# Two attention stacks: even and odd heads' scores in turn, transposed attention outputs from values held on column halves

## The chip, the cores and the metric

The kernel runs on one core of a Trainium2 chip. The metric is the device time of one execution in microseconds, as the median of several; one execution was also taken with the profiler, and its trace is what is read below.

## The reference

Two blocks follow each other on one sequence of 256 tokens and 1024 channels, each with two layers. A layer of the first block is a feed-forward network, a mixer and a second feed-forward network; a layer of the second block is a mixer of four branches and a feed-forward network. Cut to the attention, which is all that the change touches:

```python
# first block, mixer: 12 heads in 3 groups of dilated causal windows, 4 stick-breaking heads; head size 64
p = jnp.exp(s - m)                                  # s = q.k / 8, masked by window and dilation
o = einsum(p, v) / denom                            # per group; lse = m + log(denom)
w_grp = softmax(stack(lses)); o_dil = sum(w_grp * outs)
w = where(past, exp(log_beta + after), 0); o_sb = einsum(w, v)
y = gate_dil * (o_dil @ w_proj_dil) + gate_sb * (o_sb @ w_proj_sb)

# second block, mixer: 8 query heads on 2 key/value heads in branches a and d
k_cmp, v_cmp = gelu(blocks @ w1) @ w2               # 15 compressed keys and values
o_a = ga0 * attend(compressed) + ga1 * attend(selected) + ga2 * attend(window)
o_b, o_c = conformer_conv(b_in), pool_mixer(c_in)
o_d = sliding window attention with one sink logit per head in the denominator
mix = sum_n sigmoid(h @ w_gate)_n * (o_n @ w_branch[n]); x = x + norm(mix @ w_o)
```

With 256 tokens the selected branch sees every causal key, so it needs no selection.

## The kernel before

Everything is held on chip but the weights, which stream from memory once. Tokens are handled as two tiles of 128 (`t` is 0 or 1). Each product with a weight matrix runs in three TensorE passes over a high and a low part of both operands (lines 184 to 186, and 204 to 219 for the feed-forward layers of the first block). `chunk` loads a piece of a weight matrix (DMA, line 107), ScalarE makes its high part `wh` (110) and VectorE its low part `wl` (111). There are six buffers for such pieces, so loads and halving run ahead of TensorE by at most six pieces.

Attention runs in plain float32. A float32 matmul is two records in the trace, a transpose, a bfloat16 matmul or a weight pass is one. Per token tile and head the steps are: a mask is added into a PSUM bank by a bfloat16 matmul with the identity (434, 538 to 542), the scores follow into the same bank (440, 483, 546, 829), VectorE takes the row maximum (442, 549), ScalarE makes the exponentials `e` with their sums (558), TensorE transposes them (155), VectorE or ScalarE copies the result to `pt`, and `pt` is the stationary operand of the product with the values (468, 500, 572), which move with 64 columns. The output lies tokens by channels, and is then scaled by the reciprocal of the sums (469, 812, 848, 856 and 857). `split_T` transposes it (155) and splits it into high and low parts for the next weight product.

Queries and keys lie with channels on partitions, two heads to a tile: an even head on the lower 64 rows of the array, an odd head on the upper 64 rows. In `attn`, called six times a layer (once for each tile in the sliding window branch `oD`, twice for each in `oA`), all even heads are served first, then all odd ones, in banks of four heads at `t` = 0 and of two at `t` = 1. In `attend1` one head of each group is served at a time.

The compressed keys come from `compress`: 16 steps of three passes (723 to 725) with 32 stationary columns; then a gelu, small transposes, a product (757), eight copies by GpSimd that lay out `hv` (764) and a product with `hv` stationary (768).

A scheduler builds the order of each engine's instructions from the code, with priorities and an estimate of durations of its own. Each engine then runs its list in order. Weight products stand between the attention steps in TensorE's list and cover the time in which VectorE and ScalarE work on a bank. PSUM has four banks for weight products (`lin`) and four for everything else (`aux`). The convolution of branch b is 240 multiply-adds on VectorE (866), and they share the stretch of the second mixer with the softmax steps and with the halving of weights.

Of the kernel before, what the change touches and what calls it, by code (L numbers as in the profile page):

```python
# [9 lines left out]
F32R = mybir.dt.float32r  # L10
# [15 lines left out]
def body(tc, ctx, I, C, out, upto=99):  # L26
# [371 lines left out]
    def attend1(qkn, vs):  # L398
        QT = [None, None]
        oTs = []  # L400
        for t in range(2):
# [25 lines left out]
            oc = unit("oc")  # L427
            for j in range(4):
                groups = [[0, 1, 2]] if t == 0 else [[0, 1], [2]]
                ps_l, mx, sm = [], stat(4), stat(4)  # L430
                for gi, gs in enumerate(groups):
                    n = len(gs) * nk * P
                    ps = aux_ps()[:, :n]
                    nc.tensor.matmul(ps, identb, dilm[t][:, gs[0]:gs[-1] + 1, :].rearrange("p g k -> p (g k)"),
                                     start=True, stop=False)
# [10 lines left out]
                V.tensor_scalar(mx[:, 2:3], mx[:, 0:1], -0.125, None, op0=OP.mult)  # L446
                pts = []
                for gi, gs in enumerate(groups):
                    n = len(gs) * nk * P
                    e = unit("e")[:, :n]  # L450
                    S.activation(e, ps_l[gi], AF.Exp, bias=mx[:, 2:3], scale=0.125, accum_out=sm[:, gi:gi + 1])
# [11 lines left out]
                if len(groups) == 2:  # L463
                    V.tensor_add(sm[:, 0:1], sm[:, 0:1], sm[:, 1:2])
                V.reciprocal(sm[:, 2:3], sm[:, 0:1])
# [8 lines left out]
            for par in range(2):  # L474
                o = par * 64
                z = aux_ps()[:, :n]
                nc.tensor.matmul(z[:, n - 256:], identb, sbm[:, None, :].to_broadcast([P, 2, P]), start=True, stop=False)
                for kt in range(nk):
                    for jj in range(2):
# [3 lines left out]
                        nc.tensor.matmul(z[:, c0:c0 + P], k_, q_, start=False, stop=(kt == nk - 1 and jj == 1))  # L483
                S.activation(es[par], z, AF.Abs)
                zs.append(z)
# [11 lines left out]
            for j in range(4):  # L497
                for kt in range(nk):
                    c0 = kt * 256 + (j // 2) * P
                    nc.tensor.matmul(po[:, j * 64:(j + 1) * 64], ws[j % 2][:, c0:c0 + P],  # L500
                                     vs[kt][:, 768 + j * 64:768 + (j + 1) * 64], start=kt == 0, stop=kt == nk - 1)
            V.tensor_copy(oc[:, 256:512], po)
            o = split_T("c", [oc])
            o1, o2 = XT(), XT()
            o1.h, o1.l, o2.h, o2.l = o.h[:2], o.l[:2], o.h[2:], o.l[2:]
# [19 lines left out]
    def attn(t, qT, kTf, vf, window, sink=None):  # L525
# [3 lines left out]
        mx, ng, dn = stat(8), stat(8), stat(8)  # L529

        def scores(h0):
            par = h0 % 2
            hs = list(range(h0, h0 + 2 * per, 2))
            n = per * nk * P
            ps = aux_ps()[:, :n]
# [619 lines left out]
```

## Time and profile before

| | us |
|---|---|
| three executions | 2177.4, 2174.1, 2173.64 |
| median | 2174.1 |
| the profiled execution's own time | 2173.62 |
| its span in the trace | 2171.8 |
| TensorE busy in the span | 2142.1 (99%) |
| VectorE busy | 1567.7 (72%) |
| ScalarE busy | 1159.0 (53%) |
| GpSimd busy | 38.7 (2%) |

Mean granted TensorE clock of the span: 0.998 of full speed. A row of the timeline gives start, duration, engine, line, operation, output and inputs, the shape and the count of records run together, and in brackets the idle time before them and what ended it. The durations of matmuls overlap, so what one costs is the distance from its start to the next start on TensorE.

### The profile page before, as it was taken

The numbers are of one execution on the slowest core, as the hardware profiler recorded it, in microseconds if no ns is written. First come the engines' busy times: TensorE is split into PE (matmuls) and PEld (weight loads), VectorE is DVE, ScalarE is ACT, GpSimd is POOL, SyncE is SP. The second block draws the span as 40 slices with busy tenths as digits, with TensorE's granted clock in tenths as the row PEclk, the third lists the DMA queues.
The fourth block names the chain that finished last, engine by engine and source line by source line (L and its number), as shares of the span: only waits on it lengthen the run. The fifth ranks groups of instructions, "written<-read, shape, count | busy, mean of one in ns | idle before, by whom it ended". The sixth has DMA issues, their size and how long they took to land.

```text
span 2171.8 us, 30964 instructions
## 1 busy us (share of the span) xinstructions
PE 2142.1 (99%) x11824; PEld 1824.8 (84%) x11824; DVE 1567.7 (72%) x2395; ACT 1159.0 (53%) x1766; POOL 38.7 (2%) x55
## 2 busy tenths in 40 slices
PE   7999999999999999999999999999999999999998
PEld 6888888888888888888887888889987888888997
DVE  6875556786677555577757997678976898577983
ACT  5654545554555455555545554456655554446652
POOL 0000000000000000000000000000000000000000
PEclk9999999999999999999999999999999999999999
DMA  8666534666666654366666632456656643355653
GB/s 252 202 193 186 193 97 139 192 192 190 192 188 187 188 191 127 118 183 185 190 188 198 200 117 78 155 172 200 192 188 191 216 140 113 107 184 175 186 179 121
DMA packets 250821, 373.86 MB, mean 172 GB/s; under 512 B 14768, under 2 KB 123696, under 8 KB 250672
## 3 DMA queue, kind: packets, MB, share of 16 engines
q1 hardware_dynamic: 250096, 371.48, 55.8%
q8 instruction: 93, 1.52, 0.3%
q0 software_dynamic: 576, 0.39, 0.1%
q14 instruction: 56, 0.46, 0.1%
HBM read 371.17 MB, written 1.05 MB: 171 GB/s over the span
## 4 chain that ended last, share of the span: by engine, by line
PE 93%; DVE 3%; issue 1%; DMA 1%; ACT 1%; POOL 1%; SPq 0%; POOLq 0%; DVEq 0%; ACTq 0%
PE lin L186 17%; PE lin L184 17%; PE lin L185 16%; PE lin L218 15%; PE lin L219 8%; PE aux L155 4%; PE lin L206 3%; PE lin L205 3%; PE lin L204 3%; PE aux L546 2%; PE aux L572 1%; DVE wl L111 1%; PE aux L440 1%; PE aux L468 1%; ACT wh L110 0%
## 5 line engine op out<-in xcount | busy, mean ns | idle before, releaser
L111 DVE TENSOR_TENSOR wl<-raw,wh 128x1024 fp32r<-128x1024 f32 (+1 forms) x688 | 835.1, 1217 | 407.5 <-ACT wh L110 399.8
L110 ACT ACTIVATE wh<-raw 128x1024 fp32r<-128x1024 f32 (+1 forms) x688 | 723.2, 1055 | 557.0 <-PE lin L186 314.1
L218 PE MATMUL lin<-x,wh 128*128 128x512 f32 x1408 | 494.9, 396 | 0.0
L219 PE MATMUL lin<-x,wl 128*128 128x256 f32 x1408 | 395.3, 281 | 0.0
L184 PE MATMUL lin<-wh,x 128*128 128x512 f32 (+2 forms) x896 | 350.0, 391 | 0.0
L185 PE MATMUL lin<-wl,x 128*128 128x512 f32 (+2 forms) x896 | 348.2, 389 | 1.5 <-DVE wl L111 1.5
L186 PE MATMUL lin<-wh,x 128*128 128x512 f32 (+2 forms) x896 | 348.2, 389 | 1.0 <-DVE rs L1057 0.8
L218 PEld LDWEIGHTS lin<-x,wh 128*128 128x128 f32 x1408 | 264.5, 188 | 61.6
L219 PEld LDWEIGHTS lin<-x,wl 128*128 128x128 f32 x1408 | 266.4, 189 | 0.5 <-DVE wl L111 0.4
L186 PEld LDWEIGHTS lin<-wh,x 128*128 128x128 f32 x896 | 168.9, 189 | 34.5 <-DVE rs L1057 1.6
L185 PEld LDWEIGHTS lin<-wl,x 128*128 128x128 f32 x896 | 168.9, 189 | 33.0 <-DVE wl L111 1.9
L184 PEld LDWEIGHTS lin<-wh,x 128*128 128x128 f32 x896 | 168.8, 189 | 32.6 <-ACT wh L110 0.4
L186 PE MATMUL lin<-wh,lo 128*128 128x512 f32 x480 | 188.6, 393 | 0.4 <-DVE lo L147 0.4
L184 PE MATMUL lin<-wh,hi 128*128 128x512 f32 x480 | 187.2, 390 | 0.0
L185 PE MATMUL lin<-wl,hi 128*128 128x512 f32 x480 | 187.0, 390 | 0.0
L205 PE MATMUL lin<-x,wh 128*128 128x256 f32 x576 | 163.2, 283 | 0.0
L206 PE MATMUL lin<-x,wl 128*128 128x256 f32 x576 | 163.0, 283 | 0.0
L204 PE MATMUL lin<-x,wh 128*128 128x256 f32 x576 | 163.0, 283 | 0.0
L205 PEld LDWEIGHTS lin<-x,wh 128*128 128x128 f32 x576 | 110.6, 192 | 0.1
L204 PEld LDWEIGHTS lin<-x,wh 128*128 128x128 f32 x576 | 110.6, 192 | 0.1
L206 PEld LDWEIGHTS lin<-x,wl 128*128 128x128 f32 x576 | 110.6, 192 | 0.0
L186 PEld LDWEIGHTS lin<-wh,lo 128*128 128x128 f32 x480 | 90.1, 188 | 19.5 <-DVE lo L147 1.3
(317 smaller groups left out, 2774.0 us busy)
## 6 DMA issues: line engine op xcount, KB each, us to landing
raw<-in_ffn_w_up_dram SPq DMA_DIRECT2D x168, 512.0 KB, 4.3
raw<-in_ffn_w_down_dram SPq DMA_DIRECT2D x132, 512.0 KB, 4.2
raw<-in_w_in_dram SPq DMA_DIRECT2D x132, 512.0 KB, 4.1
raw<-in_ffn_w_gate_dram SPq DMA_DIRECT2D x88, 512.0 KB, 4.4
raw<-in_w_gate_dram SPq DMA_DIRECT2D x64, 512.0 KB, 3.8
raw<-in_w_branch_dram SPq DMA_DIRECT2D x32, 512.0 KB, 4.4
raw<-in_w_out_dram SPq DMA_DIRECT2D x16, 512.0 KB, 4.4
raw<-in_nsa_cmp_w_dram SPq DMA_DIRECT2D x16, 512.0 KB, 4.3
```

Of the source, the lines that this page charges most:

```text
L110: S.activation(wh, raw, AF.Copy)
L111: V.tensor_sub(wl, raw, wh.bitcast(F32))
L155: nc.tensor.transpose(p[:, i * P:(i + 1) * P], s, ident)
L184: nc.tensor.matmul(ps, xt.h[k], w[0], start=start, stop=False)
L185: nc.tensor.matmul(ps, xt.h[k], w[1], start=False, stop=False)
L186: nc.tensor.matmul(ps, xt.l[k], w[0], start=False, stop=stop)
L204: nc.tensor.matmul(o, wh, xh, start=k == 0 and i % 2 == 0, stop=False)
L205: nc.tensor.matmul(o, wh, xl, start=False, stop=False)
L206: nc.tensor.matmul(o, wl, xh, start=False, stop=k == 7 and i % 2 == 1)
L218: nc.tensor.matmul(o, wh, x, start=k == 0, stop=False)
L219: nc.tensor.matmul(o[:, :T], wl, x[:, :T], start=False, stop=k == 7)
L546: nc.tensor.matmul(pv[:, i, kt * P:(kt + 1) * P], q_, kTf(kt, h), start=False, stop=(i == per - 1 and kt == nk - 1))
```

## The change

Scores: even and odd heads get a bank each at the same time, and their matmuls are issued in turn (attention of both blocks and the compressed scores). A bank holds the same heads as before.

Values: the product is turned round. A head's or key head's 64 value columns are stationary, on the lower or the upper 64 columns of the array, and the transposed probabilities move. In `attn` one such matmul serves the four query heads of a key head with 512 moving columns; in `attend1` one serves one head, with 128. The output lies channels by tokens, and `split` alone makes the operand of the next weight product; the transposes of `oc`, `od` and `oa` go. The three parts of branch a add up in one PSUM bank, as the value product of the compressed part becomes four of 128 columns.

Scaling: the probabilities are multiplied by gate and reciprocal of the sum on VectorE after the exponential and before the transposes; the scaling of the outputs goes.

Compressed keys: high and low parts of the inputs stand side by side as 64 stationary columns, so two passes do for three; their sum is taken after the transposes by VectorE, the gelu is done by ScalarE when it writes `hv`, so GpSimd's copies go; the block moves behind the keys' transposes of tile 0. The rows of `w_branch_2` for branches a and d are put in the new order on the host, before the launch.

```diff
-            oc = unit("oc")
-            for j in range(4):
-                groups = [[0, 1, 2]] if t == 0 else [[0, 1], [2]]
-                ps_l, mx, sm = [], stat(4), stat(4)
...
+                    pss = [aux_ps()[:, :n] for _ in js]
...
-                        h = gg * 4 + j
...
-                            nc.tensor.matmul(ps[:, c0:c0 + P], qk(h, False, t), qk(h, True, kt), start=False,
-                                             stop=(gg == gs[-1] and kt == nk - 1))
-                    V.tensor_reduce(mx[:, gi:gi + 1], ps, op=OP.max, axis=AX.X)
-                    ps_l.append(ps)
+                            for ps, j in zip(pss, js):
+                                h = gg * 4 + j
+                                nc.tensor.matmul(ps[:, c0:c0 + P], qk(h, False, t), qk(h, True, kt), start=False,
+                                                 stop=(gg == gs[-1] and kt == nk - 1))
...
+                    V.tensor_scalar(e, e, sm[:, 2:3], None, op0=OP.mult)
...
-                            pts.append((u[:, c0:c0 + P], vs[kt][:, h * 64:h * 64 + 64]))
...
-                po = aux_ps()[:, :64]
-                for i, (a, b) in enumerate(pts):
-                    nc.tensor.matmul(po, a, b, start=i == 0, stop=i == len(pts) - 1)
-                V.tensor_scalar(oc[:, j * 64:(j + 1) * 64], po, sm[:, 2:3], None, op0=OP.mult)
+                            pts.append((vs[kt][:, h * 64:h * 64 + 64], u[:, c0:c0 + P]))
...
+                js = (2 * jp, 2 * jp + 1)
+                pts = [probs(j, *r) for j, r in zip(js, scores(js))]
+                if po is None:
+                    po = aux_ps()[:, :256]
+                for i in range(len(pts[0])):
+                    for par in range(2):
+                        nc.tensor.matmul(po[par * 64:par * 64 + 64, jp * P:(jp + 1) * P], *pts[par][i],
+                                         start=i == 0, stop=i == len(pts[0]) - 1)
+            ob = big("c", "hl", F32R)
+            hi, lo = ob[:, 0:512], ob[:, 512:1024]
+            split(po, hi[:, 0:256], lo[:, 0:256])
...
-            V.tensor_copy(oc[:, 256:512], po)
-            o = split_T("c", [oc])
...
+                        nc.tensor.matmul(po[par * 64:par * 64 + 64, jj * P:(jj + 1) * P], vs[kt][:, v0:v0 + 64],
+                                         ws[par][:, c0:c0 + P], start=kt == 0, stop=kt == nk - 1)
+            split(po, hi[:, 256:512], lo[:, 256:512])
...
+            for i in range(per):
                 for kt in range(nk):
-                    nc.tensor.matmul(pv[:, i, kt * P:(kt + 1) * P], q_, kTf(kt, h), start=False,
-                                     stop=(i == per - 1 and kt == nk - 1))
+                    for par, pv in enumerate(pvs):
+                        h = h0 + 2 * i + par
+                        q_ = qT[par * 64:par * 64 + 64, (h // 2) * P:(h // 2 + 1) * P]
+                        nc.tensor.matmul(pv[:, i, kt * P:(kt + 1) * P], q_, kTf(kt, h), start=False,
+                                         stop=(i == per - 1 and kt == nk - 1))
...
+            V.reciprocal(f[:, hh], dn[:, hh])
+            if gate is not None:
+                V.tensor_tensor(f[:, hh], f[:, hh], gate[:, hh], op=OP.mult)
+            for sl, ev in r:
+                V.tensor_tensor(ev, ev, f[:, sl][:, :, None].to_broadcast([P, per, nk * P]), op=OP.mult)
+
+        def turned(g, kt):
+            u = unit("pt")
+            pt = transposed([es[4 * g + r][:, kt * P:(kt + 1) * P] for r in range(4)])
...
-                    nc.tensor.matmul(po[:, h * 64:h * 64 + 64], u[:, c0:c0 + P], vf(kt, h), start=kt == 0, stop=kt == nk - 1)
...
+        us = {}
+        for h0 in range(0, 8, 2 * per):
+            scores(h0)
+        for kt in range(nk):
+            for g in range(2):
+                us[g, kt] = turned(g, kt)
+        for kt in range(nk):
+            for g in range(2):
+                nc.tensor.matmul(po[g * 64:(g + 1) * 64], vf(kt, g), us[g, kt], start=first and kt == 0,
+                                 stop=last and kt == nk - 1)
...
-            split(A, ah, al)
...
+                split(A[:, q * 256:(q + 1) * 256].rearrange("p (s n) -> p s n", s=8), v[:, :, 0], v[:, :, 1])
+                ahl += [x[:, i * 64:(i + 1) * 64] for i in range(8)]
...
-                    a = slice(s * 32, (s + 1) * 32)
-                    nc.tensor.matmul(o, ah[:, a], ws[i][0], start=s == 0, stop=False)
-                    nc.tensor.matmul(o, ah[:, a], ws[i][1], start=False, stop=False)
-                    nc.tensor.matmul(o, al[:, a], ws[i][0], start=False, stop=s == 15)
+                    nc.tensor.matmul(o, ahl[s], ws[i][0], start=s == 0, stop=False)
+                    nc.tensor.matmul(o, ahl[s], ws[i][1], start=False, stop=s == 15)
...
-                G.tensor_copy(hv5[:, hf, a], hg[:, 64 + hf * 32:96 + hf * 32].rearrange("p (g n) -> p g n", g=2)
-                              [:, :, None, :].to_broadcast([P, 2, 2, 16]))
...
+                hr = unit("hr")[0:64, :]
+                S.activation(hr, hps, AF.Copy)
...
+                V.tensor_tensor(hg4, h4[:, :, 0], hg4, op=OP.add)
...
+                        S.activation(hv5[:, hf, a], hg[:, 64 + hf * 32:96 + hf * 32].rearrange("p (g n) -> p g n", g=2)
+                                     [:, :, None, :].to_broadcast([P, 2, 2, 16]), AF.Gelu_apprx_tanh)
+                S.activation(hk, hk, AF.Gelu_apprx_tanh)
...
-            V.reciprocal(dn, dn)
-            od = unit("od")
-            V.tensor_tensor(h8(od), h8(po), bc(dn), op=OP.mult)
-            oD.append(split_T("b", [od]))
+            po = aux_ps()
+            attn(t, qT, lambda kt, h: dkT[half_of(h), kt * 256 + (h // 4) * P:kt * 256 + (h // 4 + 1) * P],
+                 lambda kt, g: vv[kt][:, 256 + g * 64:256 + (g + 1) * 64], True, po, True, True,
+                 sink=sink)
+            oD.append(split_O(po))
...
-            for par in range(2):
-                ps = aux_ps()[:, :64].rearrange("p (i n) -> p i n", i=4)
-                for i in range(4):
+            pss = [aux_ps()[:, :64].rearrange("p (i n) -> p i n", i=4) for _ in range(2)]
+            for i in range(4):
+                for par, ps in enumerate(pss):
...
+            V.tensor_tensor(s8, s8, f[:, :, None].to_broadcast([P, 8, 16]), op=OP.mult)
...
-            ops = aux_ps()
-            nc.tensor.matmul(ops, pT, vblk, start=True, stop=True)
-            oa = unit("oa")
-            V.tensor_tensor(h8(oa), h8(ops), bc(f), op=OP.mult)
+            po = aux_ps()
+            for r in range(4):
+                nc.tensor.matmul(po[:, r * P:(r + 1) * P], vblk[:, r * P:(r + 1) * P], pT,
+                                 start=r == 0, stop=False)
             for i in range(2):
-                po, dn = attn(t, qT, lambda kt, h: kT[kt][half_of(h), (2 * i + h // 4) * P:(2 * i + h // 4 + 1) * P],
-                              lambda kt, h: vv[kt][:, i * 128 + (h // 4) * 64:i * 128 + (h // 4 + 1) * 64], False)
-                f = stat(8)
-                V.reciprocal(f, dn)
-                V.tensor_tensor(f, f, sg[t][:, 8 + 8 * i:16 + 8 * i], op=OP.mult)
-                tmp = unit("ot")
-                V.tensor_tensor(h8(tmp), h8(po), bc(f), op=OP.mult)
-                V.tensor_add(oa, oa, tmp)
-            oA.append(split_T("b", [oa]))
+                attn(t, qT, lambda kt, h: kT[kt][half_of(h), (2 * i + h // 4) * P:(2 * i + h // 4 + 1) * P],
+                     lambda kt, g: vv[kt][:, i * 128 + g * 64:i * 128 + (g + 1) * 64], False, po, False, i == 1,
+                     gate=sg[t][:, 8 + 8 * i:16 + 8 * i])
+            oA.append(split_O(po))
...
+    wb = g("w_branch_2").reshape(L, 4, 2, 4, 64, 1024)
+    wb = np.stack([wb[:, n].transpose(0, 2, 1, 3, 4) if n in (0, 3) else wb[:, n].reshape(L, 4, 2, 64, 1024) for n in range(4)], axis=1)
```

The scheduler keeps the turn of even and odd heads only where it finds both banks free. On TensorE, in the sliding window scores of tile 0 (layer 0 of the second block; `aux` are the banks, `dkT` and `qT` keys and queries; one row is one matmul), before:

```order
L185 MATMUL lin_11676<-wl_11673,x_9996 128x512
L186 MATMUL lin_11676<-wh_11672,x_9996 128x512
L546 MATMUL aux_11027<-dkT_10813,qT_11017 128x128 x4
L546 MATMUL aux_11042<-dkT_10813,qT_11017 128x128 x4
L184 MATMUL lin_11676<-wh_11672,x_9996 128x512
```

and now:

```order
L186 MATMUL lin_11562<-wh_11558,x_9972 128x512
L578 MATMUL aux_10979<-dkT_10739,qT_10967 128x128
L578 MATMUL aux_10981<-dkT_10739,qT_10967 128x128
L578 MATMUL aux_10979<-dkT_10739,qT_10967 128x128
L578 MATMUL aux_10981<-dkT_10739,qT_10967 128x128
L578 MATMUL aux_10979<-dkT_10739,qT_10967 128x128
L578 MATMUL aux_10981<-dkT_10739,qT_10967 128x128
L578 MATMUL aux_10979<-dkT_10739,qT_10967 128x128
L578 MATMUL aux_10981<-dkT_10739,qT_10967 128x128
L184 MATMUL lin_11562<-wh_11558,x_9972 128x512
```

Four even matmuls and then four odd ones have become four pairs, in the same place between two weight products.

On TensorE, in the second pair of banks of the selected branch, tile 1, of the same layer (`kT` are the keys of both tiles; line 571 is the mask), now:

```order
L571 MATMUL aux_11387<-swm,identb 128x2x128
L578 MATMUL aux_11387<-kT_10749,qT_11317 128x128
L578 MATMUL aux_11387<-kT_10785,qT_11317 128x128
L578 MATMUL aux_11387<-kT_10749,qT_11317 128x128
L578 MATMUL aux_11387<-kT_10785,qT_11317 128x128
L184 MATMUL lin_11976<-wh_11928,x_9737 128x512
...
L571 MATMUL aux_11389<-swm,identb 128x2x128
L578 MATMUL aux_11389<-kT_10749,qT_11317 128x128
L578 MATMUL aux_11389<-kT_10785,qT_11317 128x128
L578 MATMUL aux_11389<-kT_10749,qT_11317 128x128
L578 MATMUL aux_11389<-kT_10785,qT_11317 128x128
```

The code issues these eight in turn; in the list the even bank's four stand apart from the odd bank's four, with eight weight products between them.

On VectorE, in the same branch and tile, before (549 and 551 maximum and its negative, 866 the convolution, 566 the copy of transposed probabilities, 853 to 857 the scaling of outputs):

```order
L549 TENSOR_REDUCE st_11446<-aux_11472 128x2
L866 SCALAR_TENSOR_TENSOR cy_10399<-cT_10398,pm_10065,cy_10399 128x226
L551 TENSOR_SCALAR st_11447<-st_11446 128x2
L566 COPY pt_11488<-aux_11483 128x512
L549 TENSOR_REDUCE st_11446<-aux_11494 128x2
L551 TENSOR_SCALAR st_11447<-st_11446 128x2
L566 COPY pt_11510<-aux_11505 128x512
L853 RECIPROCAL st_11538<-st_11448 128x8
L854 TENSOR_TENSOR st_11538<-st_11538,sg_10788 128x8
L856 TENSOR_TENSOR ot_11541<-aux_11460,st_11538 128x512
```

and now (584 and 586 maximum and its negative, 602 and 604 reciprocal and gate, 606 the scaling, 914 the convolution, 612 the copy):

```order
L602 RECIPROCAL st_11360<-st_11359 128x4
L914 SCALAR_TENSOR_TENSOR cy_10375<-cT_10374,pm_10041,cy_10375 128x232
L604 TENSOR_TENSOR st_11360<-st_11360,sg_10736 128x4
L584 TENSOR_REDUCE st_11357<-aux_11389 128x2
L606 TENSOR_TENSOR e_11375<-e_11375,st_11360 128x512
L606 TENSOR_TENSOR e_11380<-e_11380,st_11360 128x512
L586 TENSOR_SCALAR st_11358<-st_11357 128x2
L111 TENSOR_TENSOR wl_12017<-raw_12014,wh_12016 128x1024
L612 COPY pt_11413<-aux_11414 128x512
```

The scaling of 512 columns has moved from behind the value product to ahead of the transposes, one for each bank, and shares VectorE's list with the convolution and the halving of weights.

## Rows read from the trace of the kernel before

**Rows 1.** Page: busy time by engine, and the chain that ended last.

```profile
PE 2142.1 (99%) x11824; PEld 1824.8 (84%) x11824; DVE 1567.7 (72%) x2395; ACT 1159.0 (53%) x1766; POOL 38.7 (2%) x55
PE 93%; DVE 3%; issue 1%; DMA 1%; ACT 1%; POOL 1%; SPq 0%; POOLq 0%; DVEq 0%; ACTq 0%
```

**Rows 2.** Timeline of TensorE (start, us, what): scores of two and eight records.

```profile
1349.44 0.48 PE L546 MATMUL aux<-kT,qT 64*128 64x128 f32 x2
1349.86 0.28 PE L542 MATMUL aux<-swm,identb 128*128 128x256 bf16 x1
1350.07 1.16 PE L546 MATMUL aux<-kT,qT 64*128 64x128 f32 x8
1351.16 0.28 PE L542 MATMUL aux<-swm,identb 128*128 128x256 bf16 x1
...
1352.45 0.50 PE L184 MATMUL lin<-wh,x 128*128 128x512 f32 x1
1352.80 0.40 PE L185 MATMUL lin<-wl,x 128*128 128x512 f32 x1
1353.04 0.39 PE L186 MATMUL lin<-wh,x 128*128 128x512 f32 x1
```

**Rows 3.** Timeline of TensorE: eight records of even heads, then eight of odd ones.

```profile
1246.70 1.71 PE L546 MATMUL aux<-dkT,qT 64*128 64x128 f32 x16
1248.34 0.50 PE L184 MATMUL lin<-wh,x 128*128 128x512 f32 x1
```

**Rows 4.** Groups by line (count, busy us, mean ns, idle before): value products.

```profile
L572 PE MATMUL aux<-vv,pt 128*128 128x64 f32 x288 | 36.1, 270 | 0.0
...
L468 PE MATMUL aux<-v,pt 128*128 128x64 f32 x144 | 19.1, 271 | 0.0
...
L500 PE MATMUL aux<-v,sw 128*128 128x64 f32 x48 | 6.7, 275 | 0.0
```

**Rows 5.** Timeline of TensorE: value products, transposes, a float32 product of 512 columns.

```profile
1345.21 1.00 PE L572 MATMUL aux<-vv,pt 128*128 128x64 f32 x8
1346.05 0.39 PE L155 MATMUL aux<-ident,e 128*128 128x128 f32 x2
1346.28 1.00 PE L572 MATMUL aux<-vv,pt 128*128 128x64 f32 x8
...
1297.19 1.02 PE L846 MATMUL aux<-vblk,cpT 128*128 128x512 f32 x2
1298.05 0.38 PE L538 MATMUL aux<-swm,identb 128*128 128x512 bf16 x1
```

**Rows 6.** Timeline of TensorE: from 128 stationary columns to 32.

```profile
1192.31 0.28 PE L186 MATMUL lin<-wh,x 128*128 128x256 f32 x1
1192.42 0.28 PE L725 MATMUL aux<-wh,cAl 128*32 128x256 f32 x1
1192.54 0.28 PE L723 MATMUL aux<-wh,cAh 128*32 128x256 f32 x1
```

**Rows 7.** TensorE's waits by line: us in total, times, longest.

```profile
PE aux L768 <- POOL hv L764: 2.3, 2, 1.3
...
PE aux L757 <- ACT hg L754: 0.6, 1, 0.6
```

**Rows 8.** Stretches: us, busy PE, PEld, DVE, ACT, POOL, then PEclk, DMA, GB/s.

```profile
1218.10:1221.50 3.40, 3.40 (x10) 2.65 (x9) 3.40 (x8) 0.00 (x0) 0.00 (x0) 0.50 0.69 255
...
1200.00:1340.00 140.00, 138.01 (x790) 113.96 (x789) 127.45 (x269) 73.20 (x156) 2.21 (x4) 0.99 0.48 148
...
260.00:340.00 80.00, 80.00 (x458) 65.01 (x457) 40.70 (x84) 40.65 (x70) 0.00 (x0) 1.00 0.36 115
```

**Rows 9.** Groups by line on VectorE: scaling of 512 columns; the convolution.

```profile
L812 DVE TENSOR_TENSOR od<-aux,st 128x512 f32<-128x512 f32 x4 | 2.8, 692 | 3.1 <-PE aux L572 2.6 <-issue 0.6
...
L866 DVE SCALAR_TENSOR_TENSOR cy<-cT,pm,cy 128x251 f32<-128x251 f32 (+17 forms) x240 | 101.4, 462 | 0.2
```

More of the change, by code (lines that the diff above doesn't have):

```diff
@@ L482, in attend1 @@
                         c0 = kt * 256 + jj * P
-                        nc.tensor.matmul(z[:, c0:c0 + P], k_, q_, start=False, stop=(kt == nk - 1 and jj == 1))
-                S.activation(es[par], z, AF.Abs)
-                zs.append(z)
+                        nc.tensor.matmul(zs[par][:, c0:c0 + P], k_, q_, start=False, stop=(kt == nk - 1 and jj == 1))
+            for par in range(2):
+                S.activation(es[par], zs[par], AF.Abs)
             S.activation(e2[:, :2 * n], e2[:, :2 * n], AF.Exp, scale=-1.0)
@@ L523, in rope_2, with attn @@
             V.tensor_tensor(o, aa, bb, op=OP.add)
[L525 removed]
+    def attn(t, qT, kTf, vf, window, po, first, last, gate=None, sink=None):
         nk = t + 1
         per = 4 if t == 0 else 2
[L529 removed]
+        mx, ng, dn, f = stat(8), stat(8), stat(8), stat(8)
+        es = {}
         def scores(h0):
[L532 to L533 removed]
             n = per * nk * P
[L535 to L565 removed]
@@ new lines, in scores @@
+            pvs = []
+            for _ in range(2):
+                pv = aux_ps()[:, :n].rearrange("p (h k) -> p h k", h=per)
+                if t == 0:
+                    nc.tensor.matmul(pv, identb, swm[:, None, P:].to_broadcast([P, per, P]), start=True, stop=False)
+                elif window:
+                    nc.tensor.matmul(pv, identb, swm[:, None, :].to_broadcast([P, per, 2 * P]), start=True, stop=False)
+                else:
+                    nc.tensor.matmul(pv[:, :, P:], identb, swm[:, None, P:].to_broadcast([P, per, P]), start=True, stop=False)
+                pvs.append(pv)
@@ new lines, in scores @@
+            for i in range(per):
+                for kt in range(nk):
+                    for par, pv in enumerate(pvs):
[3 more added lines that the diff above has]
+                                         stop=(i == per - 1 and kt == nk - 1))
+            r = []
+            for par, pv in enumerate(pvs):
+                hs = list(range(h0 + par, h0 + 2 * per, 2))
+                sl = slice(h0 + par, h0 + par + 2 * per - 1, 2)
+                V.tensor_reduce(mx[:, sl], pv, op=OP.max, axis=AX.X)
+                if sink is None:
+                    V.tensor_scalar(ng[:, sl], mx[:, sl], -0.125, None, op0=OP.mult)
+                else:
+                    V.scalar_tensor_tensor(mx[:, sl], mx[:, sl], 0.125, sink[:, sl], op0=OP.mult, op1=OP.max)
+                    V.tensor_scalar(ng[:, sl], mx[:, sl], -1.0, None, op0=OP.mult)
+                e = unit("e")[:, :n]
+                ev = e.rearrange("p (h k) -> p h k", h=per)
+                for i, h in enumerate(hs):
+                    S.activation(ev[:, i], pv[:, i], AF.Exp, bias=ng[:, h:h + 1], scale=0.125, accum_out=dn[:, h:h + 1])
+                r.append((sl, ev))
+                for i, h in enumerate(hs):
+                    es[h] = ev[:, i]
@@ L799, in half_of, with split_O @@
             return slice((h % 2) * 64, (h % 2) * 64 + 64)
+        def split_O(po):
+            b = big("b", "hl", F32R)
+            split(po, b[:, :512], b[:, 512:])
+            xt = XT()
+            xt.add(b[:, :512], b[:, 512:])
+            return xt
         oD = []
@@ L831, in mixer2 @@
                                      start=i == 0, stop=i == 3)
+            for par, ps in enumerate(pss):
                 V.tensor_tensor(sc[:, par], ps, cmpm[t][:, None, 0:16].to_broadcast([P, 4, 16]), op=OP.add)
@@ L1102, in constants @@
     row = np.arange(P)
-    c["hsel"] = ((2 * ((row // 16) % 4) + row // 64)[:, None] == np.arange(8)[None, :]).astype(f)
+    c["hsel"] = ((2 * ((row // 16) % 4) + row // 64)[:, None] == np.array([0, 4, 1, 5, 2, 6, 3, 7])[None, :]).astype(f)
     cnt = np.stack([np.minimum(np.arange(T) + 1, w) for w in (2, 4, 8, 16)]).astype(f)
```

161 lines of the change are left out of this document (71 added, 90 removed).

## The prediction

> **What bounds the kernel now.** The page comes first: TensorE is busy for 99% of the span and makes up 93% of the chain that ended last [rows 1]. So time taken off TensorE's list comes off the end, as long as no other engine then makes TensorE wait. The timeline of TensorE is read next, for what a visit to an attention step costs from its start to the next start. Two score records take 0.42 us to the next start, eight take 1.09 [rows 2]: 0.11 a record and 0.20 for the visit. The neighbours lose too: the weight product after the scores has 0.35 to the next start, the one after it 0.24, and the 256 columns of a mask ahead of them take 0.21 [rows 2], where 256 columns in other places take 0.11 [rows 6]. I put the neighbours at 0.2 a visit. Third, the waits of TensorE, and the stretches of the two mixers, for how much room VectorE has there.
>
> **Scores.** Before: 544 records (272 matmuls of two) in 72 visits, 72×0.20 + 544×0.11 = 74.2 us. In eight visits an odd head's matmuls follow an even one's directly. Such a visit of 16 records would be 1.96 by the formula and takes 1.64 [rows 3], so the two row halves ran beside each other for about 0.3 where they met; eight times that leaves 71.6. This is the only place where the trace shows what the change is about: the halves of the array work at once when neighbours in the list use different halves. After the change the list has 58 visits, and of the 272 matmuls 92 pairs stand in turn, and 88 matmuls alone, as the scheduler split many pairs. I take a pair at the price of one matmul, 0.22: 180×0.22 + 58×0.20 = 51.2, that is **-20.4**. Bounds: a pair may cost two matmuls, which gives +20 on this. Fourteen visits fewer spare their neighbours 0.2 each: **-2.8**.
>
> **Value products.** Before: 288, 144 and 48 records [rows 4] at 0.84 for eight, 0.105 each [rows 5]: 50.4 us. After: in `attn` 36 matmuls of 512 moving columns, two records of 0.43 each as in the product of 512 [rows 5], 0.87 a matmul; in `attend1` 72 and 24 matmuls of 128 columns, 0.22 each. If neighbours on different column halves run at once as the row halves do, they need 24, 44 and 16 such times: 24×0.87 + 44×0.22 + 16×0.22 = 34.1, that is **-16.3**. If they follow one another it is 31.3 + 15.8 + 5.3 = 52.4, two more than before. No row shows two column halves at once; the nearest, the row halves [rows 3], is for the first, and I take it. Entering a tile of fewer columns has a row: from 128 stationary columns to 32 the distances stay 0.11 and 0.12 [rows 6], so the 46 visits cost 0; their bound is the score visit's 0.4, that is 18. The Trainium skill (TensorEngine Tiling (Array Packing), Tiling Modes, Key Properties) says that changing the tiling mode drains the engine. The score visits agree with 0.20 and the neighbours' 0.2, the column rows don't; by the rule all 46 visits would pay and the time would be some 2148.
>
> **What goes without a question.** The transposes of `oc`, `od` and `oa`: 48 (four blocks, two tiles, two layers, three outputs) at 0.23 for two [rows 5], **-5.5**. One of three passes of `compress`: 64 at 0.115 [rows 6], **-7.4**; 64 stationary columns in the place of 32 are loaded under the running product. The compressed value product becomes 16 matmuls of 128 columns, 3.5, where 8 records of 512 columns took 3.4: 0. GpSimd's copies of `hv`: TensorE waited 2.3 us for them in two layers and 0.6 for `hg` [rows 7], and soon after the first of these the granted clock stood at 0.50 (1.2 GHz of 2.4) for 3.4 us [rows 8], which loses 1.7. The new block has the gelu on ScalarE and lies behind tile 0's key transposes, with weight products to cover it: **-4.6**. The splits of `po` on ScalarE and VectorE stand in for those of the transposed outputs, one for one: 0. The host's order of `w_branch_2` costs nothing in the execution, and its pieces have the same size.
>
> **Sum on TensorE:** -20.4 - 2.8 - 16.3 - 5.5 - 7.4 - 4.6 = **-57.0**.
>
> **What is given back.** The second mixer's stretch has VectorE at 127.5 us busy of 140 [rows 8]; the first mixer's has 40.7 of 80, so there nothing is charged. Of the 57 some 17 lie in each layer's second mixer stretch (scores 8, value products 5, transposes 2, the wait 2), so TensorE's list there shrinks from 140 to about 123. VectorE's list grows: 18 scalings of `e` a layer at 0.69 (a 512 column product with a factor for each row block [rows 9]), less 12 operations of that size on the outputs, is +4, so 131. What lies too much is convolution (240 steps at 0.46 [rows 9]) that may run later, as branch b is used last, and the new list does put 14 more of a layer's 120 steps behind the first maximum of branch a. But each list is in order, and a step of the convolution or a halving of weights stands between reciprocal, scaling and copy, and TensorE's transposes wait for those. I charge 7 a layer, about 131 less 123, with bounds of 0 (the whole surplus moves later) and 12 (18×0.69, every scaling on the path): **+14**, 0 to 24. Also behind VectorE's scalings in its list are the `wl` halves of weights; six pieces run ahead, which covers a delay of a few us.
>
> **Result:** the profiled execution's own time is 2173.6, 0.5 under the median of 2174.1. 2173.6 - 57.0 + 14 = 2130.6. I forecast **2130**.
>
> **Rivals.**
> 1. *The column halves follow one another.* Then the 16.3 go and 2 are added, TensorE's sum is -39, and as VectorE has more room the charge falls to about 5: **2140**. For it: no row shows them at once, and both halves take the same 128 rows. Against it: loads are busy 84% of the span beside 99% of matmuls [rows 1], nearly all on the same rows, so sharing rows forbids no overlap of a load and a product. The Trainium skill (TensorE: Matmul & The Clock Gate, Part 3, The mechanism) says that a weight load overlaps running matmuls only when the row group differs; taken strictly, that is this rival, and the overlap in the trace speaks against so strict a reading.
> 2. *Row halves in turn gain nothing.* The overlap of [rows 3] may be only that of one switch, and a change of half at each matmul may cost what it gives. Then the change doesn't do what it says: -57 + 20, with a charge of 8: **2145**. With rival 1 as well, about 2158.
> 3. *VectorE becomes the bound of the second mixer.* Maximum, negative, exponential, reciprocal, gate, scaling, transposes, copy, product is a longer chain than before, and there are two `aux` banks fewer to hide it while a pair of score banks and `po` are held. At 15 to 27 us a layer it gives **2147 to 2171**. For it: 91% busy VectorE [rows 8]. Against it: half of that list is convolution.
> 4. *Slower: TensorE stands still before transposes, and its clock falls.* The scaling stands between exponential and transposes in each pair of score banks, 18 in the second mixers and 8 in the first. Where TensorE stood 0.6 + 1.3 us in the compressed keys' block, the clock fell to half for 3.4 us [rows 7, 8], 3.6 us for such a place. At all 26 places it is 94 us, 37 over what is saved: **2210**. It decides from 16 places on (57/3.6). Against it: weight products stand between scores and transposes in the list, and the waits of before name no transposes of `e`.
>
> **How the numbers follow.** Forecast 0.57; rival 1 0.19; rival 2 0.07 (with 1 as well, a part of it); rival 3 0.10; rival 4 0.07, of which 0.02 with about 16 places, near no change. The range: below, the charge of 0 gives 2117, and a clock or visits a little better 2112; above, it takes in rivals 1 and 2, both together, and half of rival 3: 2160. A measurement of this kernel can tell about 0.2% (4 us) from no change: faster 0.93, same 0.02, slower 0.05, the last two being rival 4.
>
> **What would show it.** Right: visits of eight matmuls in turn (lines 578, 443) take about 1.1 us and not 1.96; two value products on 512 columns (line 625), neighbours in the list, take 0.9 and not 1.75; lines 762 and 763 keep 0.115; no wait for GpSimd in the compressed keys' block; TensorE's waits grow to some 15 us and name line 606, 612 or 584. Wrong: distances of 0.43 between all four records of a pair (rival 1), 0.11 between all records in turn (rival 2), a VectorE stretch at 98% with TensorE's waits of 30 us or more (rival 3), or slices of TensorE's clock at half in the mixers (rival 4).

## The result and the profile after

The changed kernel takes 2142.4 us (median of four, 2141.05 to 2144.48); the kernel before, timed beside it, 2175.75. The ratio is 0.984, with a 95% interval from 0.982 to 0.987. The profiled execution's own time is 2142.4 and its span 2140.7, 31.1 less than before. The forecast was 2130, with a range of 2112 to 2160: the sign and the range held, and 12 us of the 43 that were forecast did not come.

The page of the changed kernel: span, busy time of each engine, and the chain that ended last.

```profile
span 2140.7 us, 30396 instructions
...
PE 2103.5 (98%) x11520; PEld 1760.2 (82%) x11520; DVE 1576.4 (74%) x2439; ACT 1159.0 (54%) x1786; POOL 34.2 (2%) x47
...
PE 88%; DVE 7%; ACT 1%; issue 1%; DMA 1%; POOL 1%; SPq 0%; POOLq 0%; DVEq 0%; ACTq 0%
```

TensorE is still the bound, though less purely so than in [rows 1]: VectorE's share of the chain went from 3% to 7%. TensorE is busy 38.6 us less, and the span is 31.1 shorter; the rest went into waits. The timeline of TensorE at three places that the prediction named (start, duration, line, operation, count):

```profile
1232.37 1.16 PE L578 MATMUL aux<-dkT,qT 64*128 64x128 f32 x16
1233.46 0.50 PE L184 MATMUL lin<-wh,x 128*128 128x512 f32 x1
...
1244.60 1.08 PE L625 MATMUL aux<-pt,vv 128*64 128x512 f32 x4
1245.61 0.50 PE L184 MATMUL lin<-wh,x 128*128 128x512 f32 x1
1245.95 0.40 PE L185 MATMUL lin<-wl,x 128*128 128x512 f32 x1
1246.19 0.40 PE L186 MATMUL lin<-wh,x 128*128 128x512 f32 x1
...
1265.83 1.07 PE L625 MATMUL aux<-pt,vv 128*64 128x512 f32 x2
1266.83 0.44 PE L155 MATMUL aux<-ident,qa 128*128 128x128 f32 x2
...
1181.44 0.28 PE L762 MATMUL aux<-wh,cAh 128*64 128x256 f32 x1
1181.57 0.28 PE L763 MATMUL aux<-wl,cAh 128*64 128x256 f32 x1
1181.68 0.28 PE L762 MATMUL aux<-wh,cAh 128*64 128x256 f32 x1
```

Sixteen score records in turn take 1.09 us from start to start, where [rows 3] had 1.64: as forecast. Four value records on both column halves take 1.01, and two on one half alone 1.00: the halves run at once, and rival 1 is out. But 1.00 for two records is 0.14 more than the 0.86 of the product of 512 columns on the whole array [rows 5], and the pass behind a visit has 0.34 to the next start, where the one after it has 0.24. `compress` keeps 0.11 to 0.13 with 64 stationary columns.

The waits of TensorE after the change (us in total, times, longest):

```profile
PE aux L155 <- DVE kd L550: 4.4, 2, 2.2
PE aux L155 <- DVE e L606: 2.6, 6, 0.8
...
PE aux L674 <- PE lin L184: 1.7, 2, 0.9
PE aux L527 <- ACT sw L519: 1.6, 2, 0.8
```

The waits of [rows 7] are gone, and the transposes of the rotated keys (`kd`) wait in their place. The stretches view of the same kernel (us, busy PE, PEld, DVE, ACT, POOL, then PEclk, DMA share, GB/s):

```profile
1200.60:1204.00 3.40, 3.34 (x11) 2.95 (x12) 3.40 (x7) 2.98 (x7) 0.00 (x0) 0.50 0.72 185
1180.00:1320.00 140.00, 136.34 (x781) 108.91 (x781) 131.33 (x278) 79.90 (x165) 0.00 (x0) 0.99 0.52 161
```

Behind the wait for the keys the granted clock is at half for 3.4 us again, as in [rows 8]. VectorE is busy 131.3 of 140 us in the second mixer's stretch. Each of the two kernels has one more such fall of 3.4 us before TensorE's list ends, behind a wait of 0.5 us for GpSimd (before at 1385.4 us, line 886; after at 1866.2 us, line 934). The second layer's wait for the keys, 2.2 us as well, has none behind it: from 1706.1 to 1709.5 us the granted clock is 1.00. So the length of the wait alone does not tell whether the clock falls.

All records of TensorE added up by kind, each from the end of the record before it to its own end, waits apart, give this account (us; e2, e3, e4 and e6 are experiments told of below; the other transposes, the masks and the remaining small products are left out, 125.5 before and 127.2 after):

| | before | after | e2 | e3 | e4 | e6 |
|---|---|---|---|---|---|---|
| scores | 71.2 | 51.1 | 61.4 | 48.5 | 39.6 | 40.5 |
| value products | 52.3 | 40.9 | 37.3 | 29.5 | 53.3 | 29.5 |
| transposes of oa, oc, od | 5.4 | 0 | 0 | 0 | 5.3 | 0 |
| compress | 22.2 | 14.6 | 14.6 | 14.6 | 14.6 | 14.6 |
| weight passes | 1865.6 | 1869.7 | 1868.8 | 1867.8 | 1866.3 | 1865.8 |
| waits | 23.0 | 30.2 | 31.4 | 28.3 | 30.5 | 30.6 |

### The profile page after: what moved, and what is told of

It is laid out like the page before. It is cut to its first block, busy times and chain, and to the rows that moved or that the text cites. A ratio compares the mean times of both kernels' runs of the same rounds, so it can differ in the third digit from the quotient of the medians.

```text
span 2140.7 us, 30396 instructions
## 1 busy us (share of the span) xinstructions
PE 2103.5 (98%) x11520; PEld 1760.2 (82%) x11520; DVE 1576.4 (74%) x2439; ACT 1159.0 (54%) x1786; POOL 34.2 (2%) x47
## 4 chain that ended last, share of the span: by engine, by line
PE 88%; DVE 7%; ACT 1%; issue 1%; DMA 1%; POOL 1%; SPq 0%; POOLq 0%; DVEq 0%; ACTq 0%
PE lin L186 15%; PE lin L185 15%; PE lin L184 15%; PE lin L218 15%; PE lin L219 8%; PE aux L155 3%; PE lin L205 3%; PE lin L206 3%; PE lin L204 3%; DVE cy L914 2%; DVE wl L111 2%; PE aux L625 1%; PE aux L578 1%; DMA raw<-in_w_in_dram 1%; PE aux L443 1%
## 5 line engine op out<-in xcount | busy, mean ns | idle before, releaser
L185 PEld LDWEIGHTS lin<-wl,x 128*128 128x128 f32 x896 | 168.7, 188 | 37.3 <-DVE wl L111 3.0
L225 ACT ACTIVATE su<-lin 128x256 f32<-128x256 f32 x176 | 65.4, 375 | 76.5 <-PE lin L219 76.5
```

The lines of the kernel that those rows point to most:

```text
L185: nc.tensor.matmul(ps, xt.h[k], w[1], start=False, stop=False)
L225: S.activation(u[:, i * T:(i + 1) * T], p[:, T:], AF.Copy)
```

## The experiments

**e1, the prices by themselves.** The theory after the first look at the trace: a visit to a column half (neighbouring matmuls in TensorE's list that all use halves of the array) has a price of its own and a price at the next pass, the halves run at once, and the stretch of [rows 6] misled because its 32 columns are no such visit.

```diff
+    probes = [
...
+        ("full2", lambda p, q: [full(p, 128) for _ in range(2)]),
+        ("low2", lambda p, q: [col(p, 0, 128) for _ in range(2)]),
...
+        ("turn2", lambda p, q: [col(p, i, 128) for i in range(2)]),
...
+        for _ in range(8):
+            for _ in range(6):
+                mm(lin, wr, xr)
+            f(p, q)
```

> Leaves out the whole computation: the input is copied to the output, and TensorE runs groups of six weight-like passes (128 stationary columns, 512 moving, fp32r) with one probe between them, eight times for each probe, in a fixed order. Read as distances from start to start at the full clock. Theory A (a visit to a column half has a price of its own, 0.14 us, and the pass behind it 0.43 in the place of 0.23; halves run at once; the tile of 32 columns of compress is free because it is no column half): two matmuls (four records) on the lower or upper half in 128 columns take 0.44 + 0.14, two in turn 0.22 + 0.14, twelve on one half 2.6 + 0.14, twelve in turn 1.3 + 0.14; of 512 columns two on one half 1.87, two in turn 1.0; the pass behind them 0.43. Passes with 32 or 64 stationary fp32r columns take 0.115 each, the next 0.23. Theory B (the halves follow one another and visits are free): twelve in turn 2.6, two of 512 columns in turn 1.74, the pass behind 0.23. For rows both expect twelve matmuls on one half 2.6 + 0.2 and in turn 1.3 + 0.2.

Timeline of the probe kernel. `full`, `low`, `turn` and `r` are outputs: whole array, lower column half, both halves in turn, fp32r passes on 32 columns; between two probes lie six passes.

```profile
45.96 0.60 PE L44 MATMUL full<-x 128*128 128x128 f32 x4
46.32 1.62 PE L44 MATMUL lin<-xr,wr 128*128 128x512 f32 x6
47.78 0.38 PE L44 MATMUL full<-x 128*128 128x128 f32 x2
...
60.61 0.65 PE L44 MATMUL low<-x 128*64 128x128 f32 x4
61.19 1.67 PE L44 MATMUL lin<-xr,wr 128*128 128x512 f32 x6
62.79 0.43 PE L44 MATMUL low<-x 128*64 128x128 f32 x2
...
95.39 0.44 PE L44 MATMUL turn<-x 128*64 128x128 f32 x4
95.75 1.66 PE L44 MATMUL lin<-xr,wr 128*128 128x512 f32 x6
97.34 0.44 PE L44 MATMUL turn<-x 128*64 128x128 f32 x4
...
111.11 2.83 PE L44 MATMUL low<-x 128*64 128x128 f32 x24
113.88 0.97 PE L44 MATMUL lin<-xr,wr 128*128 128x512 f32 x3
...
145.94 1.53 PE L44 MATMUL turn<-x 128*64 128x128 f32 x24
147.40 0.96 PE L44 MATMUL lin<-xr,wr 128*128 128x512 f32 x3
...
243.59 0.62 PE L44 MATMUL r<-xr,wr 128*32 128x256 f32 x4
244.05 1.55 PE L44 MATMUL lin<-xr,wr 128*128 128x512 f32 x6
245.43 0.63 PE L44 MATMUL r<-xr,wr 128*32 128x256 f32 x4
```

From probe to probe it is 1.82 us with four records on the whole array, 2.18 with the same four on one half, and 1.95 with two on each half in turn. So a visit costs 0.36 with its neighbour, and taking turns saves 0.23 on the four records. The upper half alone gives 2.18 too. Twenty-four records take 2.77 on one half and 1.46 in turn: at once, as theory A has it. The same probes on row halves give 2.87 on one half and 1.54 in turn, as expected, and four records on one row half 2.23 from probe to probe, 0.41 more than on the whole array. Passes in fp32r on 32 columns cost no visit, 1.84 in all for 0.46 of their own. Theory B is out, and the step from [rows 6] to the value products was wrong in kind.

**e2, the scores' turns undone.** The edit is shown for `attn`; the other three places where scores are issued in turn are edited likewise.

```diff
-            for i in range(per):
-                for kt in range(nk):
-                    for par, pv in enumerate(pvs):
+            for par, pv in enumerate(pvs):
+                for i in range(per):
+                    for kt in range(nk):
```

> The scores of a pair of banks are issued even head first, then odd head, everything else as in the changed kernel. The order has 240 times of 0.22 in 60 score visits (180 in 58 in the changed kernel) and 78 times in 38 visits of value products (84 in 46). Theory A (a score visit 0.20 and 0.2 at the neighbour, a column visit 0.14 and 0.2): scores +13.6, value products -5.0, neighbours -1.2: 2142.4 + 7.4 = 2150. Theory C (turns gain nothing on the path, the gain is in other parts): 2137 to 2142.

Measured: 2148.9 us, ratio 0.989 (0.987 to 0.990), 6.5 over the changed kernel. The scores went from 51.1 to 61.4 (+10.3, where theory A had +13.6) and the value products from 40.9 to 37.3, since their visits got fewer. Theory C is out and theory A holds: the turns work and lie on the path.

**e3, the value products of a call put together.** Each product's matmuls stand in TensorE's list where their operands become ready, so the scheduler made 46 visits of one to eleven matmuls out of them. Here the one whose operand is made last is issued first (shown for `attn`; the products of the first block are edited likewise).

```diff
-        for kt in range(nk):
-            for g in range(2):
-                nc.tensor.matmul(po[g * 64:(g + 1) * 64], vf(kt, g), us[g, kt], start=first and kt == 0,
-                                 stop=last and kt == nk - 1)
...
+        todo = [(g, kt) for kt in range(nk - 1, -1, -1) for g in (1, 0)]
+        with tc.issue_after(product(*todo[0]).ins):
+            for g, kt in todo[1:]:
+                product(g, kt)
```

> The changed kernel with the value products of one call put behind one another on TensorE: the product that needs the last made operand is issued first, the others stand behind it. By the order the visits to column halves fall from 46 to 24 and their times from 84 to 66, score visits 58 to 56 and times 180 to 170. Theory A (visits are what the value products lost): value products 40.5 to 29.6, scores -2.6, neighbours -4.8, in all -18.3: 2124. Theory D (the loss is VectorE's chain, which TensorE would wait for instead): the waits of TensorE grow by what the visits give, 2137 to 2142.

Measured: 2123.6 us, ratio 0.977 (0.975 to 0.978), 18.8 under the changed kernel. The value products went from 40.9 to 29.5, scores by 2.6, weight passes by 1.9 and waits by 1.9. The groups by line show it (count, busy us, mean ns), here of the changed kernel:

```profile
L625 PE MATMUL aux<-pt,vv 128*64 128x512 f32 x72 | 25.5, 616 | 0.2 <-ACT pt L614 0.2
...
L488 PE MATMUL aux<-pt,v 128*64 128x128 f32 x144 | 13.0, 281 | 0.0
```

and the same two groups of e3:

```profile
L633 PE MATMUL aux<-pt,vv 128*64 128x512 f32 x72 | 18.1, 609 | 0.0
...
L489 PE MATMUL aux<-pt,v 128*64 128x128 f32 x144 | 9.6, 278 | 0.0
```

The same 72 and 144 records cost 10.8 us less, with nothing changed but where they stand and in which order. Theory D is out for this part: the waits fell instead of growing.

**e4, the value part undone.**

```diff
-                nc.tensor.matmul(po[g * 64:(g + 1) * 64], vf(kt, g), us[g, kt], start=first and kt == 0,
-                                 stop=last and kt == nk - 1)
...
+                    nc.tensor.matmul(po[:, h * 64:h * 64 + 64], us[g, kt][:, r * P:(r + 1) * P], vf(kt, g), start=kt == 0, stop=kt == nk - 1)
...
+            V.tensor_tensor(h8(od), h8(po), bc(f), op=OP.mult)
+            oD.append(split_T("b", [od]))
```

> The changed kernel with the value part undone: probabilities stationary, values moving with 64 columns, outputs scaled afterwards and transposed, branch weights in the old order; the scores in turn and the compressed keys as changed. By the order the scores stand in 142 times and 42 visits (180 and 58 in the changed kernel), as banks come free sooner. Theory A (turned values save little, since 46 visits at 0.34 eat what the halves give): scores -11.6 and neighbours of scores -3.2, value products 50.4 + transposes 5.4 for 40.5 + 9.2, +6; -9 in all, and some 3 of TensorE's waits for the scaling go: 2130. Theory B' (the forecast's price of the value products, free visits): +22 for values and transposes and -15 for scores: 2149.

Measured: 2143.6 us, ratio 0.986 (0.985 to 0.988). Theory A missed by 13.6, and B' by 5. By the account above the scores fell by 11.5, as expected, and values and transposes rose by 12.4 + 5.3, where A had 9.9 + 5.4. The weight passes fell by 3.4 only: A charged 0.2 for the neighbour of each visit, but in the changed kernel only 26 of the 46 value visits and 36 of the 58 score visits have a weight pass next (0.20 more than its usual distance, on average). And the waits did not fall. What stands: as built, the value part as a whole is worth nothing that can be told from noise (1 us by the medians, and the intervals of 0.984 and 0.986 overlap). It saves 17.7 on values and transposes, and by the order that it leads to it takes 11.5 from the scores' pairs and some 3 at weight passes.

**e5, no scaling of the probabilities.**

```diff
-                    V.tensor_scalar(e, e, sm[:, 2:3], None, op0=OP.mult)
...
-            for sl, ev in r:
-                V.tensor_tensor(ev, ev, f[:, sl][:, :, None].to_broadcast([P, per, nk * P]), op=OP.mult)
```

> Leaves out the multiplication of the probabilities by reciprocal and gate (36 products of 512 columns and 24 smaller ones on VectorE), all else as in the changed kernel. By the order the scores stand in 168 times and 54 visits (180 and 58) and the value products in 80 times and 42 visits (84 and 46), as banks come free sooner. Theory A (the scaling costs what TensorE is seen to wait for it, 2.6 us, and the visits that the list loses by it): scores -3.4, value products -2.7, neighbours -0.8, waits -2.6: 2133. Theory D (VectorE is the bound in the second mixer, so that its 30 us of scaling lie on the path to a good part): 2115 to 2125.

Measured: 2134.4 us, ratio 0.981 (0.980 to 0.983). D is out: taking 28.5 us off VectorE (1576.4 to 1547.9 on the page) gave 8, part of it through another order. Theory A's time of 2133 holds, its parts only roughly: by the same account as above the scores fell by 2.7 (forecast 3.4) and the waits by 1.9 (2.6), the value products rose by 1.2 where a fall of 2.7 was forecast, and the weight passes fell by 4.4 (0.8), as fewer of them stand behind a visit (44 for 62).

**e6, products joined and pairs kept.** On top of e3, in the second block:

```diff
-            for i in range(per):
...
+            with tc.issue_after(lead.ins):
+                for i in range(per):
```

> The joined value products of e3, and in the second block the scores of a pair wait in TensorE's list until both banks are free, so that all stand in turn: 144 times in 44 visits where e3 has 170 in 56. Theory A: scores 48.5 to 40.5, twelve visits' neighbours at 0.15, -1.8, in all -9.8: 2113.8. Theory E (holding a pair back until its second bank is free makes TensorE wait or moves the weight products that covered the steps): TensorE's idle time grows by 5 to 10 and the time is 2119 to 2124.

Measured: 2116.4 us, ratio 0.973 (0.971 to 0.974). The scores' 8 came in full; the waits grew by 2.3. TensorE's waits in e6:

```profile
PE aux L155 <- DVE e L616: 6.6, 10, 1.0
PE aux L155 <- DVE kd L559: 3.7, 2, 2.4
```

The wait for scaled probabilities rose from 3.1 in e3 to 6.6. So A is right in the main and E to a smaller extent.

**e7, e8 and e9, the keys' transposes later.** In e7 (from the changed kernel) and e8 (from e6) the code of the rotation, the transposes and the compressed keys' block moves behind the products for `qd`; in e9 (from e6, shown here) the rotation stays:

```diff
+            kds.append((kd, dd))
+
+        for name, c0, lst in (("qd", 1304, qd),):
...
+        for t in range(2):
+            kd, dd = kds[t]
```

> The changed kernel with the code of the keys' rotation, their transposes and the compressed keys' block written behind the products for the queries of branch d, so that some 100 weight passes lie between the keys' products and their transposes on TensorE. Theory A (the wait for the rotated keys, 2.2 us in each layer, took the place of the wait for GpSimd, and the clock's fall behind it, 1.7 us once, is the old one in a new place): -4.4 - 1.7, visits and times nearly the same (-2): 2134. Theory F (what comes next in that chain is as late, so another wait takes its place): 2139 to 2142, with the transposes of the keys no longer among TensorE's waits.

> The orders of e6 and e7 together. Theory A: 2113.8 - 6 = 2108. Theory F or E for either part: 2113 to 2120.

> The order of e6, with the keys' rotation left where it was on VectorE and only their transposes and the compressed keys' block written behind the products for the queries of branch d. Theory A (the transposes of the keys need only be late against the rotation, which e7 and e8 moved along): the wait for the rotated keys, 3.7 us, and the clock's fall behind it, 1.7 us, go: 2116.4 - 5.4 = 2111. Theory F (another wait takes their place): 2115 to 2117.

Measured: e7 2138.8 (ratio 0.983, 0.981 to 0.985), e8 2115.0 (0.972, 0.971 to 0.974), e9 2116.0 (0.973, 0.972 to 0.975). In e7 and e8 the wait stayed, 4.1 and 4.4 us, as the rotation on VectorE had moved along (tile 0's `kd` is written at 1215.7 us in e7, at 1199.9 in the changed kernel); e7 was no test of the wait, and its time can't be told from the changed kernel's. In e9 the wait for `kd` is gone, the profiled execution has no fall of the clock in the mixers, and the time is still that of e6. TensorE's waits in e9:

```profile
PE lin L185 <- DVE wl L111: 4.5, 8, 1.2
PE aux L827 <- ACT hr L824: 2.9, 2, 1.5
```

The low parts of weights (1.5 in e6) and the compressed keys' block are now late in its place. Theory F holds for this block. The runs point to the arrival of the weights as what sets the time there; ScalarE's waits in e9 from 1160 to 1215 us begin with

```profile
ACT wh L110 <- DMA raw<-in_w_in_dram: 7.7, 9, 1.6
```

but no run changed that arrival, so this stays open.

**e10, the visit's price by type.**

```diff
+        ("bfull", lambda p, q: [mm(p[:, :256], wb, xb[:, :256]) for _ in range(4)]),
+        ("blow", lambda p, q: [colb(p, 0, 256) for _ in range(4)]),
...
+        ("fthirty", lambda p, q: [n32(p, 128) for i in range(2)]),
+        ("fninety", lambda p, q: [n96(p, 128) for i in range(2)]),
```

> Leaves out the whole computation, as e1; probes of other types between six weight-like passes each. Open after e1: fp32 products on 64 columns pay a visit, fp32r passes on 64 columns do not. Theory G (the price belongs to fp32 on fewer than 128 columns, whatever the half): bf16 halves pay nothing, fp32 on 32 and on 96 columns pays as on 64, 0.58 for four records and 0.43 for the next pass. Theory H (the price belongs to matmuls that name a half of the array, which fp32r passes don't): bf16 on either half pays 0.14 and 0.2 more than on all columns, fp32 on 96 columns pays nothing (four records 0.44, next 0.23). Passes on 64 rows in fp32r are open: with a row price 0.115 each plus 0.2 and 0.2, without it 0.46 for four.

The timeline of e10 (`b` is bf16, `f` fp32 on 32 or 96 columns, `rrow` fp32r on 64 rows):

```profile
34.99 0.61 PE L48 MATMUL bfull<-xb,wb 128*128 128x256 bf16 x4
35.36 1.64 PE L48 MATMUL lin<-xr,wr 128*128 128x512 f32 x6
36.84 0.61 PE L48 MATMUL bfull<-xb,wb 128*128 128x256 bf16 x4
...
49.86 0.62 PE L48 MATMUL blow<-xb,wb 128*64 128x256 bf16 x4
50.41 1.65 PE L48 MATMUL lin<-xr,wr 128*128 128x512 f32 x6
51.99 0.62 PE L48 MATMUL blow<-xb,wb 128*64 128x256 bf16 x4
...
116.95 0.62 PE L48 MATMUL fthirty<-x 128*32 128x128 f32 x4
117.50 1.67 PE L48 MATMUL lin<-xr,wr 128*128 128x512 f32 x6
119.11 0.62 PE L48 MATMUL fthirty<-x 128*32 128x128 f32 x4
...
134.03 0.60 PE L48 MATMUL fninety<-x 128*96 128x128 f32 x4
134.39 1.64 PE L48 MATMUL lin<-xr,wr 128*128 128x512 f32 x6
135.87 0.60 PE L48 MATMUL fninety<-x 128*96 128x128 f32 x4
...
163.56 0.73 PE L48 MATMUL rrow<-xr,wr 64*128 64x256 f32 x4
164.23 1.64 PE L48 MATMUL lin<-xr,wr 128*128 128x512 f32 x6
165.80 0.62 PE L48 MATMUL rrow<-xr,wr 64*128 64x256 f32 x3
```

From probe to probe: bf16 1.85 on the whole array and 2.13 on a half; fp32 2.16 on 32 columns and 1.84 on 96; fp32r on 64 rows 2.24, of which four passes at 0.115 would be 0.46 and six at 0.23 1.38, so that 0.40 is the visit. Theory G is out, since bf16 pays and 96 columns don't. H fits all of these, and rows pay in fp32r too. Only that it is the naming of a part of the array that counts is argued from them, not seen.

## Why the prediction was right or wrong

Right, by its own terms: the scores (-20.4 forecast, -20.1 measured), the transposes of the outputs (-5.5, -5.4), the third pass of `compress` (-7.4, -7.6), and that both kinds of halves run at once. Rival 1 is out by e1, rival 2 by e1 (row halves, 1.54 for 2.87) and e2. Rival 3 is out by e5. Rival 4 did not come: the waits for scaled probabilities are 2.6 us in all, and none has the clock fall behind it.

**The step that failed is the price of a visit to a column half**, which the prediction set to 0 from [rows 6], with 0.4 as a bound. It measures 0.14 for the visit itself: 46 of them are 6.4, and 34.1 + 6.4 = 40.5 for the value products, where 40.9 was measured (-11.4 for -16.3). The 26 weight passes behind such visits lose 0.20 each, 5.3 more (the 0.20 counted from end to end, as in the table). The Trainium skill's rule (TensorEngine Tiling (Array Packing), Tiling Modes, Key Properties) that a change of mode drains the engine, which the prediction weighed and set aside, is borne out by e1 as far as a price goes, 0.36 a visit; that the engine drains is not seen in any run. The sum of 2148 by that rule was too high, mainly since not each visit has a weight pass next. The rows that spoke against it were of fp32r passes, which pay nothing for fewer columns (e1).

**The neighbours of the scores**, -2.8, did not come. The fourteen visits that went had no weight pass behind them: 36 weight passes follow directly on a score visit in the kernel before and 36 in the changed one, each with 0.20 more.

**The compressed keys' block**, -4.6, turned into a wait for `kd` of 4.4 in place of 2.9, with the same fall of the clock: +1.5. The prediction named weight products as the cover, and TensorE's list does put three passes there, about 0.7 us, where the rotation came 2.2 us later still. By e9 the gain could not be had by moving the transposes alone.

**The charge of +14** for VectorE was too high. VectorE's work grew as forecast (1567.7 to 1576.4, 8.7 for 8), but little of it held TensorE up. TensorE's other waits rose by 5.7 (7.2 in all, less the 1.5 of the keys' block), and 2.6 of these name line 606; 1.6 lie in the first block (line 527), where nothing was charged. This made up for part of the misses: 4.9 (values), 5.3 + 2.8 (neighbours), 6.1 (keys' block), less 8.3 here, is 10.8 of the 12. That the forecast came so near is luck to that extent: the misses on TensorE alone are 19 us.

What the prediction did not ask: what the new value products do to the scores' pairs. In e4, without them, the scores stand in 142 steps of 0.22 us (a matmul alone or a pair at once) and 42 visits, in the changed kernel in 180 and 58. The value part in its present order gives up there what it saves, and so is worth some 1 us of the 33, not told from none; joined, as in e3, the same operations give another 19, and with the score pairs kept together too, as in e6, 26. The best versions run, e6, e8 and e9, take 2115 to 2116 us, 0.973 of the time before.

## What to carry to other kernels

Count visits, not only matmuls: entry to and exit from a half of the array cost together as much as three small records (0.36 us in e1 against 0.11), so small products belong behind one another, and where a scheduler sets the order, the one that becomes ready last should go first. Before a price is taken from a row, see that type and shape are those of the new operation. Where a stall is taken away, look for what else arrives at that place, for which the waits of the neighbouring operations in the trace are the first hint.

## What the runs showed of the hardware that was not expected

Between weight passes, a visit costs 0.28 to 0.36 us with fp32 or bf16 matmuls of 64 stationary columns, on either half (e1, e10), and with fp32 of 32 columns (e10). With fp32r passes of 32 or 64 columns (e1) and fp32 of 96 (e10) it costs 0.02 us at most. On 64 rows both fp32 (e1) and fp32r (e10) pay about 0.4. Column halves with the same 128 rows ran at once, 24 records in 1.46 us for 2.77. The Trainium skill (TensorE: Matmul & The Clock Gate, Part 3, The mechanism) lets a load overlap running matmuls only where the row group differs; here all row groups were shared, loads were busy for 1.29 of those 1.46 us beside matmuls that were busy all the time, and the measurement decides.
